# First norm's modulation formed per channel tile, and the first four FFN column tiles accumulated contraction-outermost

## The chip, the cores and the metric

One core of a Trainium2 chip runs the whole program in one launch. The metric is device time in microseconds (us) of that core; the time before is the median of three runs.

## The reference

A two-layer backbone over 512 tokens of width 1024: 256 context tokens, modulated by the condition `c_ctx`, then 256 latent tokens, modulated by `c`. Each layer is a half-step SwiGLU FFN, three parallel mixers (S5, attention, RWKV-7) with gates and an output projection, and a second half-step FFN. What matters here is the very first sub-layer:

```python
m = silu(cond) @ w_ada + b_ada              # nine vectors of 1024 per layer and condition
def norm_modulate(x, w, shift, scale):
    return rms_norm(x, w) * (1.0 + scale) + shift
def ffn_half(x, norm_w, shift, scale, gate, w1, w3, w2):
    h = norm_modulate(x, norm_w, shift, scale)
    return x + 0.5 * gate * ((silu(h @ w1) * (h @ w3)) @ w2)
```

The first norm needs two of the nine vectors (shift and scale, 2048 columns of `w_ada`, 8 MB) before the first product can be formed. The other seven are formed later, as background work.

## The kernel before

Activations lie channel-major: 8 tiles of 128 channels on the partitions, 512 tokens in the free dimension (0 to 255 context, 256 to 511 latent). All large products use float32r operands split in a high and a low part, so one product of a 128x128 weight tile is three matmuls (`mm3`, L889 to L891: high*high, high*low, low*high). Weights come as units of 128x512 numbers (256 KB) through the SP queue (`wunit`, L876; load L882); ScalarE makes the high part `wh` (L884), VectorE the low part `wl` (L885). Four raw and seven split buffers rotate.

The FFN (`ffn`, L1081) runs over two halves of 11 column tiles. For a column tile `f` it forms `p1` (w1) and `p3` (w3), each by `dense` (L896): one PSUM bank, 8 channel tiles in turn, 24 matmuls. Then Silu, a product and a split into `ghi`, `glo` (L1102 to L1105). After 11 tiles come 8 output tiles against w2 (33 matmuls each). Background work is handed out by `side()` once per column tile: from the fourth on, 56 modulation tiles of VectorE (`ada_tile`, L948: a 128x1024 row tile times the condition, summed, L962, once per condition) and 62 steps of the S5 preparation (`s5_prep`, VectorE, POOL, ScalarE). The first load of that preparation (`s5lam`, L496) is tied to the load of the last weight unit of its column tile.

Within one engine the order of instructions is fixed when the program is built: a planner goes through the program and places what is ready by its own estimate, the program's order breaking ties (`schedule_with_timeline_sim=True`). Each engine then works strictly in that order.

The start, in `ffn` with `before`:
- `first` (L1178) spreads the two conditions over all partitions by matmuls with 2 rows (`cbp`, L1190) and Silu (`cb`, L1191).
- `norm_first` (L1006) squares the 8 tiles of `xT` on ScalarE (L1013), adds them up on POOL (L1014), sums over channels with four matmuls of one column (`nss`, L1016), takes the root on POOL (`rs`, L1019), spreads it by transposes (`nrb`, L1021), copies it (L1023), and multiplies all 8 tiles by it on POOL (L1024).
- `ada_start` (L976) forms the modulation vectors: the scale of channel tiles 0 to 3 and then 4, 5 on TensorE, the two conditions as stationary columns and `w_ad0` moving (`ap`, L989), then back to channel-major (L997, L999); the shift of tiles 0 to 5 and both vectors of 6 and 7 on VectorE (10 row tiles, 20 instructions `aj`, L962).
- Then per channel tile: modulation (L1029, two instructions), high part (L1030) on ScalarE, low part (L1031) on VectorE.
- The first weight units are held back behind the load of row tile 6 (`K.after`, L959, L882).

PSUM has four pairs of banks: `mm` and `pa` for the dense products, `px` and `pc` for the rest.

Of the kernel before, what the change touches and what calls it, by code (L numbers as in the profile page):

```python
# [20 lines left out]
def rwkv_load(K, L):  # L21
# [8 lines left out]
    # derived: 1-mu, .5mu, .5w0, .5a0, .5ka, 1-.5ka , rkblk  # L30
# [22 lines left out]
class Rwkv:  # L53
    """One layer of the RWKV mixer. Channels of two heads (q: pair, par: which of the pair) lie on the
    128 partitions; direction 1 is kept in reversed token order within each 256-token half."""
    def __init__(s,K,L,W,last):
# [6 lines left out]
        # tags of the serial part: a tag's buffers are handed out in the order of the program  # L63
# [3 lines left out]
        s.ZL=[p.tile([128,2,4,4,128],F32,name=f"ZL{L}{par}",tag=f"ZL{par}") for par in range(2)]   # half, dp, slot, cols  # L67
        s.AM=p.tile([128,2,4,4,128],F32,name=f"AM{L}",tag="AM")
        s.BT=p.tile([128,2,4,4,128],F32,name=f"BT{L}",tag="BT")
        s.et=p.tile([128,2,2,2,4],F32,name=f"et{L}",tag="et")     # half, d, q, slot  # L70
        s.kd={}
        s.XV={}; s.hops=[]     # s.hops: last matmul of each step of the serial part

    def feat(s,t,ps):
        """f tile t (r0 r1 k0 k1 v0 v1 wa g) from PSUM: centred shift and lerp"""
# [3 lines left out]
        h0=1 if s.last and t in (0,1,7) else 0; C=slice(h0*256,512)     # the last layer reads r and g of the latent tokens only  # L79
# [19 lines left out]
    def kknorm(s):  # L99
        """kk = k*k_k, normalised per head, times 1/sqrt(2)"""  # L100
# [22 lines left out]
    def xv(s,sl):  # L123
        """tile that holds states and values of slot sl, with its values filled in"""
# [4 lines left out]
        if sl//2 not in s.XV:  # L129
            X=s.f4([128,2,2,2,2,64],f"XV{L}{sl//2}")      # slot, par, d, q, v  # L130
# [30 lines left out]
    def piece(s,hf,d,q,th,ta):  # L161
        """chunk matrices of one half, direction and head pair: ZL, AM, BT, et"""
# [4 lines left out]
        sv=s.last and hf==0     # only the state is wanted  # L167
# [12 lines left out]
        T2=s.f2([128,2,256],f"T2{nm}")       # (beta, k), token  # L180
# [11 lines left out]
        BK=s.f2([128,4,2,64],f"BK{nm}")        # slot, (beta,k) or (k,beta), token  # L192
# [22 lines left out]
        # token-major [beta;k]*exp(tot)  # L215
# [32 lines left out]
    def solve_b(s,hf):  # L248
        """inverses of 32x32 blocks, then of the 64x64 blocks, into AM"""
# [184 lines left out]
def exp_acc(nc,pool,out,x,n,nm):  # L434
    """out = exp(x) to float32 rounding, x any, [128,n] tiles"""
# [13 lines left out]
    # 2^k through the exponent field  # L449
# [6 lines left out]
def sincos_acc(nc,pool,sn,cs,x,n,nm):  # L456
    """sin and cos of x by reduction to [-pi,pi], half angle Taylor and one doubling"""
# [18 lines left out]
    V.tensor_mul(s,s,r)          # sin(x/2)  # L476
# [8 lines left out]
def cmul(E,ore,oim,ar,ai,br,bi,t1,t2):  # L485
    """o = a*b complex with engine E elementwise; outs may alias nothing"""
# [3 lines left out]
def s5_prep(K,L,pool):  # generator; each step is one piece of background work  # L490
    """Discretised matrices of layer L, written to DRAM scratch per group of two pairs."""
# [931 lines left out]
```

## Time and profile before

| | |
|---|---|
| runs | 2367.77, 2358.55, 2364.77 us |
| median | 2364.77 us |
| span of the profiled execution | 2365.0 us (no time of its own is listed beside the span) |
| TensorE busy | 2248.8 us, 95% of the span |
| VectorE, ScalarE, POOL busy | 67%, 45%, 29% |
| mean granted TensorE clock | 0.956 |
| moved by DMA | 363.46 MB, mean 154 GB/s |

Times in the profile are counted from the start of the span. The granted clock is a share of 2.4 GHz (0.50 is 1.2 GHz); where no change has been recorded yet it stands at 1.00. A float32 matmul appears as two MATMUL rows, a float32r matmul as one. A merged row "start, length, engine, line, operation, xN" covers N instructions that follow one another on their engine.

### The profile page before, as it was taken

The numbers are of one execution on the slowest core, as the hardware profiler recorded it, in microseconds if no ns is written. First come the engines' busy times: TensorE is split into PE (matmuls) and PEld (weight loads), VectorE is DVE, ScalarE is ACT, GpSimd is POOL, SyncE is SP. The second block draws the span as 40 slices with busy tenths as digits, with TensorE's granted clock in tenths as the row PEclk, the third lists the DMA queues.
The fourth block names the chain that finished last, engine by engine and source line by source line (L and its number), as shares of the span: only waits on it lengthen the run. The fifth ranks groups of instructions, "written<-read, shape, count | busy, mean of one in ns | idle before, by whom it ended". The sixth has DMA issues, their size and how long they took to land.

```text
span 2365.0 us, 40987 instructions
## 1 busy us (share of the span) xinstructions
PE 2248.8 (95%) x14438; PEld 1931.5 (82%) x14438; DVE 1578.8 (67%) x3212; ACT 1057.8 (45%) x2469; POOL 692.9 (29%) x1182
## 2 busy tenths in 40 slices
PE   7998979998999999899999999999999889998999
PEld 3876767876789999688888888888887778888999
DVE  7885469569854776876647656535547985687655
ACT  4445453343335554553223345525335424665554
POOL 5039960045511323783000002402003453231000
PEclk8999989999869999999999999999999978999999
DMA  7565467354332264445535525535524543265664
GB/s 255 169 204 172 133 203 239 117 165 132 92 98 81 95 209 140 155 169 193 170 118 178 154 88 187 189 118 174 174 74 140 163 113 109 75 212 191 178 190 131
DMA packets 216578, 363.46 MB, mean 154 GB/s; under 512 B 50482, under 2 KB 85426, under 8 KB 216244
## 3 DMA queue, kind: packets, MB, share of 16 engines
q1 hardware_dynamic: 214356, 360.09, 48.7%
q8 instruction: 113, 1.85, 0.3%
q10 hardware_dynamic: 2016, 0.76, 0.1%
q14 instruction: 93, 0.76, 0.1%
HBM read 320.90 MB, written 39.86 MB: 153 GB/s over the span
## 4 chain that ended last, share of the span: by engine, by line
PE 71%; DVE 10%; POOL 8%; issue 5%; DMA 3%; ACT 3%; SPq 0%; DVEq 0%; POOLq 0%; ACTq 0%
PE p L891 15%; PE p L890 15%; PE p L889 15%; PE pg L891 3%; PE pg L889 3%; PE pg L890 3%; POOL s5w L487 1%; DVE s L962 1%; POOL s5u L487 1%; POOL s5u L488 1%; POOL s5w L488 1%; PE pv L256 1%; PE pS L261 1%; PE pq L890 1%; DVE s5w L661 1%
## 5 line engine op out<-in xcount | busy, mean ns | idle before, releaser
L885 DVE TENSOR_TENSOR wl<-wr,wh 128x512 fp32r<-128x512 f32 (+1 forms) x568 | 385.7, 682 | 361.5 <-ACT wh L884 331.6
L884 ACT ACTIVATE wh<-wr 128x512 fp32r<-128x512 f32 (+1 forms) x568 | 347.5, 617 | 544.2 <-PE p L890 460.4
L889 PE MATMUL p<-hhi,wh 128*128 128x512 f32 (+1 forms) x1440 | 518.2, 363 | 15.4 <-ACT wh L884 11.5
L890 PE MATMUL p<-hlo,wh 128*128 128x512 f32 (+1 forms) x1440 | 520.8, 363 | 1.5 <-DVE hlo L1071 1.2
L891 PE MATMUL p<-hhi,wl 128*128 128x512 f32 (+1 forms) x1440 | 520.4, 362 | 0.6 <-DVE wl L885 0.6
L889 PEld LDWEIGHTS p<-hhi,wh 128*128 128x128 f32 x1440 | 274.2, 192 | 58.7 <-ACT wh L884 13.6
L891 PEld LDWEIGHTS p<-hhi,wl 128*128 128x128 f32 x1440 | 275.6, 192 | 43.8 <-DVE wl L885 2.4
L890 PEld LDWEIGHTS p<-hlo,wh 128*128 128x128 f32 x1440 | 275.6, 191 | 42.9 <-DVE hlo L1071 1.9
L962 DVE SCALAR_TENSOR_TENSOR s<-ad,cb 128x1024 f32<-128x1024 f32 x224 | 275.9, 1234 | 2.6
L889 PE MATMUL p<-ghi,wh 128*128 128x512 f32 (+1 forms) x704 | 249.5, 355 | 4.1 <-ACT ghi L1104 4.1
L890 PE MATMUL p<-glo,wh 128*128 128x512 f32 (+1 forms) x704 | 249.4, 355 | 0.5 <-DVE glo L1105 0.5
L891 PE MATMUL p<-ghi,wl 128*128 128x512 f32 (+1 forms) x704 | 249.1, 354 | 0.0
L891 PE MATMUL pg<-hhi,glpg 128*128 128x256 f32 x512 | 158.2, 309 | 9.1 <-DVE glpg L874 8.4
L889 PE MATMUL pg<-hhi,ghpg 128*128 128x256 f32 x512 | 156.3, 305 | 0.1
L889 PEld LDWEIGHTS p<-ghi,wh 128*128 128x128 f32 x704 | 133.7, 190 | 22.9 <-ACT ghi L1104 5.0
L890 PE MATMUL pg<-hlo,ghpg 128*128 128x256 f32 x512 | 152.1, 297 | 0.0
L890 PEld LDWEIGHTS p<-glo,wh 128*128 128x128 f32 x704 | 133.6, 190 | 19.1 <-DVE glo L1105 0.9
L891 PEld LDWEIGHTS p<-ghi,wl 128*128 128x128 f32 x704 | 133.5, 190 | 18.1 <-issue 0.2
L873 ACT ACTIVATE ghpg<-wrpg 128x256 fp32r<-128x256 f32 x176 | 72.0, 413 | 123.3 <-PE pg L890 101.7
L874 POOL TENSOR_TENSOR glpg<-wrpg,ghpg 128x256 fp32r<-128x256 f32 x88 | 69.2, 789 | 171.5 <-ACT ghpg L873 161.4
L891 PEld LDWEIGHTS pg<-hhi,glpg 128*128 128x128 f32 x512 | 104.7, 205 | 16.6 <-DVE glpg L874 10.2
L889 PEld LDWEIGHTS pg<-hhi,ghpg 128*128 128x128 f32 x512 | 104.7, 204 | 6.1 <-issue 0.7
(716 smaller groups left out, 4494.1 us busy)
## 6 DMA issues: line engine op xcount, KB each, us to landing
wr<-w SPq DMA_DIRECT2D x480, 256.0 KB
ad<-w_ada SPq DMA_DIRECT2D x138, 512.0 KB
wrpg<-w_g SPq DMA_DIRECT2D x96, 256.0 KB
wr<-w SPq DMA_DIRECT2D x64, 192.0 KB
s5tab<-s5tabd SPq DMA_DIRECT2D x16, 640.0 KB
s5tabd<-s5tb SPq DMA_DIRECT2D x8, 768.0 KB
wrpf<-w_f SPq DMA_DIRECT2D x24, 256.0 KB
gd<-gt SPq DMA_DIRECT2D x24, 256.0 KB
```

The costliest lines, as they stand in the source:

```text
L256: for m in range(16): h=nc.tensor.matmul(pv[R,m,:],AMv[H,m,c:c+32],T[H,m,:],start=True,stop=True)
L261: for m in range(16): h=nc.tensor.matmul(pS[R,m,:],VT[R,m,:],D[R,m,:],start=True,stop=True)
L487: E.tensor_mul(t1,ar,br); E.tensor_mul(t2,ai,bi); E.tensor_sub(ore,t1,t2)
L488: E.tensor_mul(t1,ar,bi); E.tensor_mul(t2,ai,br); E.tensor_add(oim,t1,t2)
L873: K.nc.scalar.activation(hi,raw,AF.Copy)
L874: (K.nc.gpsimd if eng=='pool' else K.nc.vector).tensor_sub(lo,raw,hi.bitcast(F32))
L884: nc.scalar.activation(hi[:,0:n],raw,AF.Copy)
L885: (nc.gpsimd if eng=='pool' or i<=K.PW else nc.vector).tensor_sub(lo[:,0:n],raw,hi[:,0:n].bitcast(F32))
L889: nc.tensor.matmul(ps,lhi,rhi,start=start,stop=False)
L890: nc.tensor.matmul(ps,lhi,rlo,start=False,stop=False)
L891: nc.tensor.matmul(ps,llo,rhi,start=False,stop=stop)
L962: nc.vector.scalar_tensor_tensor(j,raw,1.0,K.cb[:,v,:],op0=ALU.mult,op1=ALU.mult,accum_out=K.M[L][:,v,ct:ct+1])
```

## The change

- `w_ad0` is repacked: 8 loads of 1 MB, one per channel tile, each with shift and scale of that tile for all 1024 rows. The 10 row tiles on VectorE are gone, and `ada_start` with them.
- New `ada_rows`: per channel tile 8 float32 matmuls with 256 moving columns. The stationary operand is 32 columns wide (two conditions, the rest zero); the products go to PSUM partitions 0, 32, 64, 96 in turn, so four groups of 32 array columns each sum a quarter of the rows. A ScalarE copy and two small matmuls against `c_sel` add the four quarters and turn them channel-major; two small VectorE instructions give shift and scale.
- The sums of squares go through TensorE for every channel tile (8 times four one-column matmuls) in place of the POOL additions.
- The norm is as in the other norms: per channel tile and condition one VectorE instruction with the spread root read from PSUM, ScalarE for the high part, VectorE for the low part. The POOL multiplication is gone.
- The products of the first two column tiles (w1 and w3 of f=0 and f=1) are formed together: four banks (`mm`, `pa`, `mm`, `pa`), channel tile outermost, 12 matmuls per channel tile. The first four weight units are loaded behind `xT` and the first `w_ad0`, the second four at channel tile 3. `K.after` is gone.

The diff, cut (it also strips comments and docstrings throughout, left out here):

```diff
-def ada_start(K,k,ct):
...
-def norm_first(K,before):
...
+def ada_rows(K,k,raw):
+    nc=K.nc; M=K.M[0]
+    ps=K.px([128,256],f"ar{k}")
+    for r in range(2):
+        for j in range(4):
+            i=r*4+j; nc.tensor.matmul(ps[j*32:j*32+32],K.ct[:,i,:],raw[:,i*256:i*256+256],start=r==0,stop=r==1)
+    row=(K.st,K.tn)[k%2][:,4096:4352]
+    nc.scalar.activation(row,ps,AF.Copy)
+    pc=K.pc([128,2,2],f"ac{k}")
+    for c in range(2): nc.tensor.matmul(pc[:,c],row[:,c*128:c*128+128],K.sel0,start=True,stop=True)
+    nc.vector.tensor_scalar(M[:,:,k],pc[:,0],K.bada[0][:,k:k+1],None,op0=ALU.add)
+    nc.vector.tensor_scalar(M[:,:,8+k],pc[:,1],K.bada1[:,k:k+1],K.nw[0][:,k:k+1],op0=ALU.add,op1=ALU.mult)
+
+def first_products(K):
...
+    for k in range(8): nc.sync.dma_start(xT[:,k],I['xT'][:,k])
+    load(0)
+    src=[I[w][0,0,f] for f in (0,1) for w in ('w1','w3')]
+    us=[[wunit(K,u[:,0:512],512)] for u in src]
+    for k in (1,2,3): load(k)
+    ps=K.mm([128,4],"nss0")
+    for k in range(8):
+        sq=p.tile([128,2,256],F32,name=f"nsq0{k}",tag="nt",bufs=2).rearrange("p a t -> p (a t)")
+        nc.scalar.activation(sq,xT[:,k],AF.Square)
+        for t in range(4): nc.tensor.matmul(ps[:,t:t+1],sq[:,t*128:(t+1)*128],K.ones1,start=k==0 and t==0,stop=k==7,skip_group_check=True)
+    ada_rows(K,0,raw(0))
...
+    pr=K.pc([128,512],"nrb0")
...
+    bank=[mm(K,f"p{'13'[i%2]}00{i//2}",alt=i%2==1) for i in range(4)]
+    for k in range(8):
+        if k==3:
+            for u,w in zip(src,us): w.append(wunit(K,u[:,512:1024],512))
+        tt=p.tile([128,2,256],F32,name=f"nt0{k}",tag="nt",bufs=2)
+        for h,v,s in ((0,1,slice(0,256)),(1,0,slice(256,512))):
+            t=tt[:,h]; a=M[:,v,8+k:9+k]; b=M[:,v,k:k+1]
+            nc.vector.scalar_tensor_tensor(t,xT[:,k,s],a,pr[:,s],op0=ALU.mult,op1=ALU.mult)
+            nc.scalar.activation(K.hhi[:,k,s],t,AF.Identity,bias=b)
+            nc.vector.scalar_tensor_tensor(K.hlo[:,k,s],t,b,K.hhi[:,k,s].bitcast(F32),op0=ALU.add,op1=ALU.subtract)
+        if k<7: ada_rows(K,k+1,raw(k+1))
+        if k+4<8: load(k+4)
+        for ps,w in zip(bank,us):
+            hi,lo=w[k//4]; j=slice(k%4*128,k%4*128+128)
+            mm3(nc,ps,hi[:,j],lo[:,j],K.hhi[:,k],K.hlo[:,k],k==0,k==7)
+    return bank
...
-def ffn(K,L,i,n0,side,before=None):
+def ffn(K,L,i,n0,side,first=False):
...
+    if first: bank=first_products(K)
...
-            if ff==0 and not n0 and not before:
+            if first and ff<2: p1,p3=bank[2*ff:2*ff+2]
+            elif ff==0 and not n0:
...
+    wa=inp['w_ada'][0][:,0:2048].reshape(8,128,2,8,128)
+    A['w_ad0']=cc(wa.transpose(3,1,0,2,4)).reshape(8,128,2048)
```

## Rows read from the trace of the kernel before

**Rows 1.** Page: part 1, part 4 (chain by engine), part 5 (weight split, mean ns).
```profile
PE 2248.8 (95%) x14438; PEld 1931.5 (82%) x14438; DVE 1578.8 (67%) x3212; ACT 1057.8 (45%) x2469; POOL 692.9 (29%) x1182
...
PE 71%; DVE 10%; POOL 8%; issue 5%; DMA 3%; ACT 3%; SPq 0%; DVEq 0%; POOLq 0%; ACTq 0%
...
L885 DVE TENSOR_TENSOR wl<-wr,wh 128x512 fp32r<-128x512 f32 (+1 forms) x568 | 385.7, 682 | 361.5 <-ACT wh L884 331.6
```

**Rows 2.** Windows of 20 us: length, then PE, PEld, DVE, ACT, POOL busy, clock, DMA, GB/s.
```profile
40.00:60.00 20.00, 17.66 (x67) 13.93 (x68) 19.95 (x40) 11.65 (x21) 1.07 (x1) 0.82 0.68 232
...
100.00:120.00 20.00, 20.00 (x89) 16.54 (x89) 19.64 (x52) 6.51 (x11) 0.00 (x0) 1.00 0.68 217
...
160.00:180.00 20.00, 16.42 (x68) 12.99 (x66) 12.49 (x27) 13.51 (x52) 18.09 (x37) 0.92 0.52 169
...
280.00:300.00 20.00, 16.32 (x70) 13.01 (x68) 6.75 (x13) 2.44 (x5) 14.14 (x34) 0.91 0.25 73
```

**Rows 3.** Groups by line, PE: first row 0 to 60 us, second 0 to 80.
```profile
L889 PE MATMUL p<-hhi,wh 128*128 128x512 f32 x23 | 9.8, 456 | 4.0 <-ACT wh L884 4.0
...
L889 PE MATMUL p<-hhi,wh 128*128 128x512 f32 x53 | 20.5, 418 | 4.0 <-ACT wh L884 4.0
```

**Rows 4.** Timeline, 0 to 60 us: start, length, engine, line, operation.
```profile
0.84 0.95 POOL L547 MEMSET s5WT<- 128x1024 f32 x1
...
3.00 7.18 PE L1190 MATMUL cbp<-cr,ident 2*128 2x512 f32 x8 [3.00 <-DMA cr<-c]
...
20.47 1.05 PE L1016 MATMUL nss<-ones,nacc 128*128 128x1 f32 x8 [1.79 <-POOL nacc L1014]
...
22.93 1.98 POOL L1019 TENSOR_TENSOR rs<-ms,mhalf 128x4 f32<-128x4 f32 x1 [2.51 <-DVE ms L1018]
...
24.96 0.65 PE L1021 MATMUL nrb<-ident,rs 128*128 128x128 f32 x4 [1.63 <-POOL rs L1019]
...
25.55 1.05 PE L999 MATMUL apc<-ident,tn 2*128 2x2 f32 x8
...
26.33 14.75 POOL L1024 TENSOR_TENSOR tn<-xT,st 128x512 f32<-128x512 f32 x8 [1.42 <-ACT st L1023]
...
33.79 2.28 DVE L962 SCALAR_TENSOR_TENSOR aj<-ad,cb 128x1024 f32<-128x1024 f32 x1
...
38.21 1.74 DVE L1031 TENSOR_TENSOR hlo<-nt,hhi 128x512 fp32r<-128x512 f32 x1
...
43.57 0.79 PE L891 MATMUL p<-hhi,wl 128*128 128x512 f32 x1 [0.63 <-DVE wl L885]
```

**Rows 5.** Windows, PE alone: length, busy, clock, DMA share, GB/s.
```profile
27.00:28.00 1.00, 1.00 (x3) 0.50 0.90 362
...
33.00:35.00 2.00, 0.00 (x0) 1.00 0.82 238
...
37.00:38.00 1.00, 1.00 (x2) 0.50 0.00 0
```

**Rows 6.** Timeline: float32 matmuls to one column group (L989) and to two (L295).
```profile
10.11 3.31 PE L989 MATMUL ap<-st,cT 128*2 128x512 f32 x4
...
14.24 1.88 PE L989 MATMUL ap<-st,cT 128*2 128x512 f32 x4 [0.82 <-DMA st<-w_ad]
...
705.68 0.69 PE L295 MATMUL p<-XV,ZL 128*64 128x64 f32 x16
```

**Rows 7.** Single lines: ns min/median/max, first and last start, forms.
```profile
L295 PE MATMUL p<-XV,ZL x256: 222/222/271, 705.7 to 2068.1; 128*64 128x64 f32 x128
...
L1064 DVE SCALAR_TENSOR_TENSOR ntf<-xT,M,nrbf x40: 466/475/481, 1028.3 to 2172.1; 128x256 f32<-128x256 f32 x40
```

**Rows 8.** Windows of 5 us, columns as in the windows of 20 us.
```profile
10.00:15.00 5.00, 4.18 (x7) 0.52 (x7) 4.33 (x4) 2.38 (x4) 3.95 (x4) 1.00 1.02 417
```

**Rows 9.** Timeline of SP, then of POOL: first load and first long run of S5.
```profile
66.63 0.43 SPq L496 DMA_DIRECT2D s5lam<-s_lam  x1
...
156.14 0.76 POOL L487 TENSOR_TENSOR s5u<-s5B,s5f 128x64 f32<-128x64 f32 x1 [9.14 <-DVE s5t L526]
```

More of the change, by code (lines that the diff above doesn't have):

```diff
@@ L946, in prods, with ada_tile @@
             mm3(K.nc,ps[:,s],h,l,hhi[:,k,s],hlo[:,k,s],k==0 and c==n0,k==nk-1 and c+w==z)
-def ada_tile(K,L,ct,vecs,fin=True):
+def ada_tile(K,L,ct,vecs):
     nc=K.nc
@@ L955, in ada_tile @@
         for v in range(2): nc.scalar.activation(K.cb[:,v,:],K.cb[:,v,:],AF.Silu)
-    if not fin and ct<2: raw=K.ff.tile([128,1024],F32,name=f"ad{L}_{ct}",tag="fs",bufs=2)
-    else: raw=K.adp.tile([128,1024],F32,name=f"ad{L}_{ct}",tag="adr",bufs=K.ADR)
-    with K.tc.issue_after(K.po) if L and ct<K.ADR else nullcontext(): i=nc.sync.dma_start(raw,K.I['w_ada'][L,ct])
-    if not fin and ct==K.CA: K.after=i.ins
+    raw=K.adp.tile([128,1024],F32,name=f"ad{L}_{ct}",tag="adr",bufs=K.ADR)
+    with K.tc.issue_after(K.po) if L and ct<K.ADR else nullcontext(): nc.sync.dma_start(raw,K.I['w_ada'][L,ct])
     for v in vecs:
-        j=K.junk if fin else K.adp.tile([128,1024],F32,name=f"aj{L}_{ct}_{v}",tag="adj",bufs=1)
-        nc.vector.scalar_tensor_tensor(j,raw,1.0,K.cb[:,v,:],op0=ALU.mult,op1=ALU.mult,accum_out=K.M[L][:,v,ct:ct+1])
-    if fin and ct%8==7:
+        nc.vector.scalar_tensor_tensor(K.junk,raw,1.0,K.cb[:,v,:],op0=ALU.mult,op1=ALU.mult,accum_out=K.M[L][:,v,ct:ct+1])
+    if ct%8==7:
         j=ct//8
@@ L974, in ada_fin @@
         nc.vector.tensor_scalar(M[:,v,s],M[:,v,s],0.5,None,op0=ALU.mult)
-def ada_start(K,k,ct):
+def ada_rows(K,k,raw):
     nc=K.nc; M=K.M[0]
-    if k not in (0,4): return
-    n=4 if k==0 else 2; w=n*128; c0=8+k; ps=K.pa([2,512],f"ap{k}")
-    for u in range(n):
-        raw=K.st[:,(k+u)*1024:(k+u)*1024+1024] if k+u<5 else K.tn[:,8:10,:].rearrange("p a t -> p (a t)")
-        if k==0 and u<2:
-            for h in (4*u,4*u+2): nc.sync.dma_start(K.xT[:,h:h+2],K.I['xT'][:,h:h+2])
-        nc.sync.dma_start(raw,K.I['w_ad0'][k+u])
-        for i in range(1024//w):
-            j=u*(1024//w)+i
-            nc.tensor.matmul(ps[:,0:w],ct[:,j,:],raw[:,i*w:i*w+w],start=j==0,stop=j==7)
-        ada_tile(K,0,k+u,(0,1),fin=False)
-    def fin(a,b,scale):
-        m=M[:,:,a:b]; sh=[128,2,b-a]
-        nc.vector.tensor_add(m,m,K.bada[0][:,a:b].unsqueeze(1).to_broadcast(sh))
-        if scale: nc.vector.scalar_tensor_tensor(m,m,1.0,K.nw[0][:,a-8:b-8].unsqueeze(1).to_broadcast(sh),op0=ALU.add,op1=ALU.mult)
-    fin(k,k+n,False)
-    row=K.tn[0:2,10,:]
-    nc.scalar.activation(row[:,0:w],ps[:,0:w],AF.Copy)
-    pc=K.pa([128,4,2],f"apc{k}")
-    for i in range(n): nc.tensor.matmul(pc[:,i,:],row[:,i*128:i*128+128],K.ident[0:2,0:2],start=True,stop=True)
-    nc.vector.tensor_copy(M[:,:,c0:c0+n],pc[:,0:n].rearrange("p i v -> p v i"))
-    fin(c0,c0+n,True)
-    if k==4:
-        for i in (6,7):
-            for c in (i,8+i): ada_tile(K,0,c,(0,1),fin=False); fin(c,c+1,c>7)
@@ L1006, in norm_first @@
-def norm_first(K,before):
-    nc=K.nc; xT=K.xT; p=K.nrm
-    before(0)
-    acc=p.tile([128,2,256],F32,name="nacc0",tag="nacc",bufs=1).rearrange("p a t -> p (a t)")
+    ps=K.px([128,256],f"ar{k}")
[6 more added lines that the diff above has]
+    for c in range(2): nc.tensor.matmul(pc[:,c],row[:,c*128:c*128+128],K.sel0,start=True,stop=True)
@@ new lines, in ada_rows @@
+    nc.vector.tensor_scalar(M[:,:,k],pc[:,0],K.bada[0][:,k:k+1],None,op0=ALU.add)
+    nc.vector.tensor_scalar(M[:,:,8+k],pc[:,1],K.bada1[:,k:k+1],K.nw[0][:,k:k+1],op0=ALU.add,op1=ALU.mult)
+def first_products(K):
+    nc=K.nc; xT=K.xT; p=K.nrm; I=K.I; M=K.M[0]
+    K.st=K.ff.tile([128,11,512],F32,name="st",tag="ghi",bufs=1).rearrange("p a t -> p (a t)")
+    K.tn=K.ff.tile([128,11,512],F32,name="tn",tag="glo",bufs=1).rearrange("p a t -> p (a t)")
+    K.ct=K.tn[:,4608:4864].rearrange("p (a b) -> p a b",a=8); K.sel0=K.tn[:,4864:4866]; K.bada1=K.tn[:,4896:4904]
+    ct=K.st[:,4608:4624].rearrange("p (a b) -> p a b",a=8)
+    nc.sync.dma_start(ct,I['cT']); nc.scalar.dma_start(K.sel0,I['c_sel'])
+    nc.gpsimd.memset(K.ct,0.0); nc.scalar.activation(K.ct[:,:,0:2],ct,AF.Silu)
+    nc.vector.tensor_scalar(K.bada1,K.bada[0][:,8:16],1.0,None,op0=ALU.add)
+    raw=lambda k: (K.st,K.tn)[k%2][:,k//2%2*2048:k//2%2*2048+2048]
+    load=lambda k: nc.sync.dma_start(raw(k),I['w_ad0'][k])
+    for k in range(8): nc.sync.dma_start(xT[:,k],I['xT'][:,k])
[4 more added lines that the diff above has]
+    ps=K.mm([128,4],"nss0")
@@ L1011, in norm_first @@
     for k in range(8):
-        sq=acc if k==0 else p.tile([128,2,256],F32,name=f"nsq0{k}",tag="nt",bufs=2).rearrange("p a t -> p (a t)")
+        sq=p.tile([128,2,256],F32,name=f"nsq0{k}",tag="nt",bufs=2).rearrange("p a t -> p (a t)")
         nc.scalar.activation(sq,xT[:,k],AF.Square)
-        if k: nc.gpsimd.tensor_add(acc,acc,sq)
-    ps=K.px([128,4],"nss0")
-    for t in range(4): nc.tensor.matmul(ps[:,t:t+1],acc[:,t*128:(t+1)*128],K.ones1,start=True,stop=True)
+        for t in range(4): nc.tensor.matmul(ps[:,t:t+1],sq[:,t*128:(t+1)*128],K.ones1,start=k==0 and t==0,stop=k==7,skip_group_check=True)
@@ L1079, in resid @@
         nc.vector.scalar_tensor_tensor(K.xT[:,m,s],(ps[1-v] if isinstance(ps,tuple) else ps)[:,s],g,K.xT[:,m,s],op0=ALU.mult,op1=ALU.add)
-def ffn(K,L,i,n0,side,before=None):
+def ffn(K,L,i,n0,side,first=False):
     nc=K.nc; I=K.I; p=K.ff
     sub=0 if i==0 else 2
-    if before:
-        K.st=p.tile([128,11,512],F32,name="st",tag="ghi",bufs=1).rearrange("p a t -> p (a t)")
-        K.tn=p.tile([128,11,512],F32,name="tn",tag="glo",bufs=1)
-        norm_first(K,before)
+    if first: bank=first_products(K)
     else: norm(K,L,sub,n0,f"f{L}{i}")
@@ L1136, in build @@
         K.ident=cst.tile([128,128],F32,name="ident")
-        K.ct=cst.tile([128,8,2],F32,name="cT")
         K.mhalf=cst.tile([128,64],F32,name="mhalf"); nc.gpsimd.memset(K.mhalf,-0.5)
@@ L1192, in first @@
                 with tc.tile_pool(name="s5p",bufs=1) as sp:
-                    ffn(K,0,0,0,mkside(weave(ada_tasks(0,range(16,72),1),prep_tasks(0,sp),22,3)),before=lambda k: ada_start(K,k,ct))
+                    ffn(K,0,0,0,mkside(weave(ada_tasks(0,range(16,72),1),prep_tasks(0,sp),22,3)),first=True)
                 after_a(0)
```

15 lines of the change are left out of this document (removed).

## Prediction

> **What bounds the kernel now.** I read the page first, then the windows, then the start by timeline. The page [rows 1]: TensorE is busy 95% of the span and is 71% of the chain that ended last, so what counts is when the products start and where TensorE waits. The windows of 20 us [rows 2] show two kinds of stretch in the first FFN. From 100 to 120 us TensorE is busy throughout, 89 matmuls in 20 us, 0.2247 us each, and VectorE runs 19.64 of 20 with the background work: both are full. From 160 us POOL is busy 18.09 of 20, TensorE loses 3.6 us there and 3.7 between 280 and 300, where it waits behind the S5 preparation.
>
> The start is the stretch that the change rewrites. The groups by line give three lines of dense products with 23 matmuls each by 60 us [rows 3], 69 in all. At 0.2247 us the 96th, the last of the first two column tiles, comes at 60 + 27 x 0.2247 = **66.1 us**. After the change the same 96 are the ones formed contraction-outermost, so the time of the 96th is the measure: what it moves, all behind it moves, if the FFN passes it on.
>
> Why they are late [rows 4]: the products that follow one another start at 43.57, though the spread root stood at 25.61. In between POOL multiplies eight tiles (14.75 us to 41.1) while VectorE shares the time, so a modulation pass of VectorE takes 2.28 us there and a low part 1.74, and each queues behind the other. The median of the runs, 2364.77, stands 0.2 under the span of 2365.0, so I work from 2365. Some 0.5%, 11.8 us, is what a measurement can tell from no change; the three runs shown lie 9.2 us apart.
>
> **Part by part.** *Removed:* 20 modulation passes of VectorE, eight POOL multiplications (14.75 us), seven POOL additions, 16 ScalarE modulations and their copies. All of it lay between 10 and 60 us, and it is what held the products back. SP issues 16 loads for xT and the modulation where it issued 20, of the same 10 MB, and the first weight units move from behind the sixth row tile to behind xT and the first 1 MB. No SP load waits for VectorE's row tiles any more.
>
> *Added, in the order in which TensorE meets it.* (a) The spreading of the conditions stays: 3.00 to 10.18 us [rows 4]. (b) The sums of squares: 8 x 4 matmuls, 64 in the profile's count. Eight of them took 1.05 us, so 64 take 8.4 us at that clock and 16.8 at half of it. The clock at the start was the lower one: four matmuls of 512 columns took 3.31 us at 10.11 and 1.88 at 14.24 [rows 6]. So TensorE is through with them between 10.2 + 8.4 = 18.6 and 27.0; ScalarE's squares and xT (2 MB at 417 GB/s [rows 8], 5 us) end well before. I take the middle, 22.8, since the rise before 14.24 came with wide matmuls that the one-column ones do not replace. (c) Mean, root and transposes: 1.98 + 0.65 [rows 4] and hand-overs, 3.0 us, VectorE now being free: 25.8. (d) The first channel tile: two VectorE instructions of 0.475 [rows 7], then ScalarE's high part and VectorE's low part of the second half, counted at the same length: 2.0 us with hand-overs. First dense product at **27.8**.
>
> (e) The modulation by TensorE: 16 matmuls of 256 columns per channel tile. In one column group 512 columns took 0.47 us (1.88 / 4), so 256 take 0.235 and 16 in series 3.8 us. With two groups alternating, 16 matmuls of 64 columns took 0.69 us [rows 6], of which 0.22 is the last one's length [rows 7]: 0.031 us from start to start, where one group by the same price gives 0.059. Two groups ran side by side; for four the bounds are 0.95 us (all four) and 3.8 (none). I take 0.95, as the trace shows no sign of a series. With it go four small matmuls at 1.05 / 8 = 0.13 [rows 4], so 1.5 us a channel tile. The page "TensorE: Matmul & The Clock Gate" of the Trainium skill (Part 3, measured speedup) gives 2.38 times for three column groups; an estimate from it for four, at the same loss, is 3.2 times and 1.2 us, which would add 1 us to the sum.
>
> (f) How many of these lie on the path: at 417 GB/s 1 MB is 2.5 us. xT is in at about 9, then the first `w_ad0` at 11.5, weights 14, and channel tiles 1 to 3 at 16.5, 19 and 21.5. TensorE has 5 us free between 22.8 and 27.8, so four of the eight are done before the first product, if the planner hoists them; it does hoist what is ready (the S5 memsets of a later column tile run at 0.84 us [rows 4]). Four remain: 6.0 us. (g) 96 products: 21.6 us. (h) The clock: it was down at 27, 37 and again until shortly after 47 in the kernel before, after stretches like 33 to 35 us without a matmul [rows 5]. Dense products ran from 43.57 and the clock rose near 47.1, half of 3.6 us lost: 1.8 us.
>
> Sum: 27.8 + 21.6 + 6.0 + 1.8 = **57.2 us**, 8.9 earlier than 66.1.
>
> *What lies beside it.* VectorE per channel tile: four instructions of 0.475, two small ones, one weight split of 0.68 [rows 1]: 3.0 us, hidden beside 2.7 us of products and 1.5 of modulation; with no modulation left to form VectorE would set the pace by 0.3 us a tile. ScalarE has two high parts, a copy and a split, less than that. DMA: channel tile 7 lands after 12 MB, at about 34 us, TensorE wants it after 50. The row copy in `ada_rows` is a new wait, ScalarE between two matmul groups, some 0.6 us; behind it on TensorE stand the products of the tile before if the planner puts them there, else 0.6 x 4 is added, 2.4 us. The root stays in one `pc` bank, the small matmuls share the other; they wait for a VectorE read of 0.2 us. Next late: the S5 preparation. Its first load is tied to the fourth column tile's weights (66.63 us, long run on POOL from 156.14 [rows 9]) and its VectorE steps lie between the background passes, so I move it with the products.
>
> Forecast: 2365.0 - 8.9 = **2356 us**. Its own bounds: (b) at full clock and no loss in (h) give 51.2 and 2350; (b) at half clock, or two groups at a time, 61 and 2360.
>
> **Rivals.** *DMA alone bounds the start.* The clock stays up from 13 us, rows overlap with one-column matmuls: last `w_ad0` 34 + its rows and norm 4 + 12 products 2.7 = 41 us, 25 earlier, 2340; between that and 2350, I name 2345. For it: DMA is full at the start, share 1.02 [rows 8]; against: 96 products after a root at 25 us do not fit before 47.
>
> *Column groups in series.* 2.85 us more for each of four rows: 68.6 us, 2367. Against it the 0.031 us above.
>
> *The gain is given back.* The time lost from 160 us hangs on POOL, busy 18.09 of 20 [rows 2]. If its chain starts at 156 as before, because VectorE at 19.64 of 20 cannot prepare it sooner, the products wait there: 2365. Against: VectorE's queue holds the same order, only earlier.
>
> *Slower: the clock stays at half through the first products.* The place is TensorE between 27 and 85 us; it decides if the products come in bursts of 12 with waits between, as each channel tile waits for its modulation. Then (b) ends at 27.0, the first product is at 32, and (e) and (g) double: 32 + 2 x 27.6 = 87 us, 21 later, 2386. For it: the first two products of the kernel before, at 37 us, ran at clock 0.50 with nothing behind them [rows 5]. Against: once rows are ahead, 12 products are 2.7 us without a gap. The same page of the Trainium skill, section "Loop structure matters more than you think", calls a load waited for in each contraction step the bad loop, since TensorE then runs cold; by that rule this case decides, and the trace bears it out only for gaps like that from 33 to 35 us.
>
> **How the numbers follow.** Forecast 0.35, a third of it below 2353; DMA bound 0.30; series 0.08; given back 0.15; half clock 0.12. Faster by over 0.5%: 0.30 + 0.12 = 0.42. Within: 0.23 + 0.08 + 0.15 = 0.46. Slower: 0.12. The range takes in the DMA bound and the series case, 2341 to 2369, and leaves out the half clock. The forecast's own range is 2350 to 2362.
>
> **What would show it.** The count of dense products by 60 us should be near 105 rather than 69. The first `nss` group should end near 23, the root's transposes near 26, the first dense product near 28. `ada_rows` matmuls should start in fours. POOL's long S5 run should start near 147. Wrong, if the 96th product is after 66, if the clock reads 0.50 between 35 and 55, if starts lie 0.2 apart within a modulation group, or if the start moves and the FFN's end does not.

## The result, and the profile after

The changed kernel takes **2384.05 us** (median of six runs, 2382.82 to 2389.09); the kernel before, beside it, 2367.38 (six runs, 2358.55 to 2379.30). The ratio is 1.0072, with an interval of 1.0047 to 1.0096: slower by 16.7 us, outside the predicted range. The profiled run took 2383.67 us with a span of 2381.9, 16.9 over the span of before.

The page of the changed kernel, its first part, against [rows 1]: TensorE has 172 MATMUL rows more (14610 for 14438) and is busy 20.4 us longer; VectorE and POOL are relieved.

```profile
PE 2269.2 (95%) x14610; PEld 1952.3 (82%) x14610; DVE 1560.6 (66%) x3199; ACT 1053.5 (44%) x2466; POOL 664.9 (28%) x1168
```

Where the 16.9 us arise is read from windows cut at the same places of the work in both: the start of the 96th, 1584th, 1800th, 4000th, 7000th, 7250th and 9000th dense product. The columns are the window, its length, busy time and instructions of PE, PEld, DVE, ACT and POOL, the granted clock, DMA share and GB/s. First the kernel before:

```profile
0.00:66.00 66.00, 49.38 (x159) 27.28 (x160) 49.23 (x77) 30.18 (x55) 30.66 (x26) 0.90 0.70 246
66.00:453.30 387.30, 357.03 (x1585) 290.95 (x1584) 282.38 (x643) 170.85 (x494) 167.21 (x372) 0.96 0.56 180
...
492.40:1067.20 574.80, 540.47 (x4249) 469.87 (x4248) 413.88 (x898) 267.00 (x605) 258.55 (x396) 0.92 0.42 131
1067.20:1739.40 672.20, 670.67 (x3118) 559.82 (x3117) 389.26 (x684) 267.13 (x613) 81.50 (x183) 1.00 0.51 158
...
1781.50:2213.90 432.40, 404.44 (x3581) 363.46 (x3580) 317.81 (x666) 220.88 (x505) 143.30 (x188) 0.92 0.48 146
```

The same windows of the changed kernel:

```profile
0.00:69.00 69.00, 64.25 (x332) 43.89 (x333) 24.64 (x64) 25.90 (x52) 3.71 (x12) 0.98 0.63 235
69.00:456.20 387.20, 355.20 (x1585) 288.86 (x1584) 282.26 (x643) 170.95 (x494) 167.28 (x372) 0.97 0.56 180
...
495.30:1068.60 573.30, 536.48 (x4249) 466.46 (x4248) 417.80 (x896) 267.12 (x607) 256.78 (x398) 0.93 0.41 132
1068.60:1740.80 672.20, 670.67 (x3117) 559.63 (x3116) 391.35 (x687) 266.32 (x612) 81.39 (x180) 1.00 0.51 158
...
1783.00:2230.60 447.60, 415.72 (x3580) 373.33 (x3580) 318.32 (x666) 221.52 (x505) 144.19 (x188) 0.88 0.46 141
```

The start loses 3.0 us where 8.9 were to be gained. The first FFN is as long as before (387.2 for 387.3), and so are the FFNs between the mixers (672.2). The mixers of layer 0 are 1.5 shorter, those of layer 1 **15.2 longer**, and the rest is equal within 0.3. So most of the loss lies 1700 us behind the change, in a stage that no line of it touches. (These are single profiles; one program profiled twice, among the experiments, has its mixers alike within 0.4 us and its 96th product 1.6 us apart.)

**The start.** The timeline of TensorE in the changed kernel (start, length, engine, line, operation, count; PEld is the loading of the stationary operand):

```profile
3.15 5.46 PE L1187 MATMUL cbp<-cr,ident 2*128 2x512 f32 x6 [3.15 <-DMA cr<-c]
8.53 3.49 PEld L1011 LDWEIGHTS nss<-ones,nsq 128*128 128x128 f32 x16 [1.50 <-issue]
8.53 3.57 PE L1011 MATMUL nss<-ones,nsq 128*128 128x1 f32 x16
12.03 2.07 PE L1187 MATMUL cbp<-cr,ident 2*128 2x512 f32 x2
14.03 3.57 PE L1011 MATMUL nss<-ones,nsq 128*128 128x1 f32 x16
17.53 1.93 PE L980 MATMUL ar<-st,tn 128*32 128x256 f32 x16
...
25.61 3.57 PE L1011 MATMUL nss<-ones,nsq 128*128 128x1 f32 x16
...
33.46 0.65 PE L1017 MATMUL nrb<-ident,rs 128*128 128x128 f32 x4
...
36.49 1.85 PE L889 MATMUL p<-hhi,wh 128*128 128x512 f32 x4
38.27 1.94 PE L980 MATMUL ar<-st,tn 128*32 128x256 f32 x16
40.14 0.50 PE L890 MATMUL p<-hlo,wh 128*128 128x512 f32 x1
```

The sums of squares come in four groups of 16 rows (two rows are one matmul) and 3.57 us, 0.223 us a row, and end at 29.2 us; the root stands on POOL at 30.6, but its transposes wait in TensorE's queue behind modulation rows until 33.46 (POOL's rows, from the same timeline):

```profile
29.54 1.01 POOL L1015 TENSOR_TENSOR rs<-ms,mhalf 128x4 f32<-128x4 f32 x1 [26.30 <-DVE ms L1014]
```

The first product starts at 36.49, against 36.9 in the kernel before; the stream of products starts at 40.1 against 43.57 [rows 4] and then carries the rows of four channel tiles between its groups of 12. The single line of the high*high products has fewer by 60 us (20 where [rows 3] has 23), and after that it does not catch up (48 by 80 us for 53). Three such lines make 60 dense products by 60 us, where the prediction looked for 105:

```profile
L889 PE MATMUL p<-hhi,wh x20: 389/397/628, 36.5 to 56.5; 128*128 128x512 f32 x20
...
L889 PE MATMUL p<-hhi,wh x48: 389/389/628, 36.5 to 79.4; 128*128 128x512 f32 x48
```

Windows of 4 us of the changed kernel show what limits it there: DMA is full until 42 us, later than the 34 reckoned, and then nearly idle up to 50 us, while TensorE, which still waits for 1.6 us between 34 and 38, is busy throughout from there on.

```profile
34.00:38.00 4.00, 2.40 (x13) 1.76 (x12) 4.00 (x13) 2.20 (x5) 0.00 (x0) 0.84 1.00 402
38.00:42.00 4.00, 4.00 (x25) 2.15 (x25) 2.25 (x6) 1.29 (x3) 0.00 (x0) 0.73 0.95 383
42.00:46.00 4.00, 4.00 (x22) 3.33 (x21) 0.60 (x3) 0.00 (x0) 0.00 (x0) 1.00 0.07 26
46.00:50.00 4.00, 4.00 (x32) 2.56 (x30) 1.79 (x6) 0.91 (x2) 0.00 (x0) 1.00 0.01 4
```

(Where no change of the clock has been recorded yet, a window shows 1.00; up to 36 us the lengths of the matmuls tell that it was the lower level.) In the stage windows above the same is seen as busy time: 332 matmuls and 64.25 of 69 us after, 159 and 49.38 of 66 before. The kernel before waited for VectorE and POOL; this one is held by TensorE's own added work.

**The mixers of layer 1.** Of the 15.2 us, 11.3 are TensorE's busy time (415.72 for 404.44, for the same number of matmuls), at a mean clock of 0.88 for 0.92, and 3.9 are waits. Windows of 10 us in the middle of the stage show the first kind, in the kernel before:

```profile
2000.00:2010.00 10.00, 10.00 (x192) 9.44 (x187) 3.52 (x7) 3.31 (x8) 4.74 (x5) 0.67 0.20 67
2010.00:2020.00 10.00, 9.99 (x133) 8.99 (x131) 7.45 (x15) 7.11 (x14) 3.45 (x3) 0.84 0.23 69
2020.00:2030.00 10.00, 10.00 (x127) 8.93 (x128) 8.00 (x15) 4.41 (x11) 4.26 (x6) 1.00 0.22 67
2030.00:2040.00 10.00, 10.00 (x127) 8.87 (x126) 6.74 (x17) 5.34 (x17) 2.04 (x3) 1.00 0.31 93
```

and in the changed one:

```profile
2000.00:2010.00 10.00, 10.00 (x141) 9.26 (x139) 3.39 (x8) 3.55 (x8) 1.76 (x2) 0.50 0.17 53
2010.00:2020.00 10.00, 9.75 (x135) 9.11 (x133) 3.50 (x7) 4.51 (x9) 4.14 (x5) 0.50 0.19 49
2020.00:2030.00 10.00, 10.00 (x107) 9.09 (x105) 4.61 (x8) 2.18 (x6) 3.47 (x4) 0.50 0.15 47
2030.00:2040.00 10.00, 10.00 (x96) 8.59 (x94) 8.53 (x16) 6.01 (x14) 3.96 (x4) 0.82 0.20 67
```

TensorE waits for nearly nothing in either, but from 2000 to 2030 the changed kernel runs at 1.2 GHz throughout. (The same window holds somewhat different parts of the stage in the two.) The instructions do not stand in the same order: of the last 11800 instructions of TensorE, 2851 stand in another place than in the kernel before, nearly all of them in the two mixers (counted in the two programs). The orders of the other engines, and which buffer of a rotation an instruction gets, move along with it. Nothing in the code there was edited. The planner that fixes the order goes by its own estimates of time, and with another start it places what is ready in the mixers differently; the experiments show that a delay of the start is enough.

### The profile page after: what moved, and what is told of

The parts are those of the page before. It is cut to its first block, busy times and chain, and to the rows that moved or that the text cites. A ratio compares the mean times of both kernels' runs of the same rounds, so it can differ in the third digit from the quotient of the medians.

```text
span 2381.9 us, 41318 instructions
## 1 busy us (share of the span) xinstructions
PE 2269.2 (95%) x14610; PEld 1952.3 (82%) x14610; DVE 1560.6 (66%) x3199; ACT 1053.5 (44%) x2466; POOL 664.9 (28%) x1168
## 4 chain that ended last, share of the span: by engine, by line
PE 74%; DVE 8%; POOL 7%; issue 4%; DMA 3%; ACT 2%; SPq 1%; DVEq 0%; ACTq 0%; POOLq 0%
PE p L889 15%; PE p L890 15%; PE p L891 15%; PE pg L891 3%; PE pg L889 3%; PE pg L890 3%; POOL s5w L487 1%; POOL s5u L487 1%; PE pS L261 1%; POOL s5w L488 1%; POOL s5u L488 1%; DVE s L959 1%; PE pv L256 1%; DVE s5w L661 1%; PE pq L890 1%
## 5 line engine op out<-in xcount | busy, mean ns | idle before, releaser
L884 ACT ACTIVATE wh<-wr 128x512 fp32r<-128x512 f32 (+1 forms) x568 | 347.0, 618 | 539.7 <-PE p L890 463.8
```

Source lines behind the costliest of these rows:

```text
L884: nc.scalar.activation(hi[:,0:n],raw,AF.Copy)
```

## The experiments

Two theories were put against each other. One: the start costs 3 us, and the planner's other order of the mixers costs the rest. The other: the new start itself costs everything (its loads, buffers or the clock), or the clock decides by itself and the order is without weight. Four kernels take both starts with both kinds of order. The planner's order is moved by a short delay ahead of the first load; nothing computed is changed by it (`xT` is overwritten by its load):

```diff
+xf=K.xT.rearrange("p a t -> p (a t)"); nc.gpsimd.memset(xf[:,0:N],0.0); nc.gpsimd.tensor_copy(K.ident,xf[:,0:128])
 nc.sync.dma_start(K.ident,I['c_ident'])
```

**After, mixers as before** (the changed kernel, N=1328; 32 of the last 11800 TensorE instructions differ from the kernel before).

> The changed kernel with one POOL memset of 1328 columns ahead of the first load, which delays the start by some 1.5 us; with it the planner puts the two mixers in the order of the kernel before. Theory A (the planner's order of the mixers makes most of the loss, the start only 2.9 us): 2367 + 1.5 + 2.9 = 2371 us, 13 less than the changed kernel without the delay. Theory B (the mixers lose at run time, through clock and transfers, whatever their order): 2384 + 1.5 = 2385 us. Both: the last product of the first FFN starts about 4.4 us after that of the kernel before.

**Before, the same delay** (N=1328; its own order of the mixers).

> The kernel before with the same memset; its mixers keep their order. Both theories: 2367 + 1.5 = 2368 to 2369 us. The difference of the run before this one to it is the price of the changed start alone, order of the mixers equal: A says 2.9 us, B says 16.

**Before, other mixers** (N=2228; 3404 of 11800 differ).

> The kernel before with a memset of 2228 columns, some 2.3 us of delay, at which the planner reorders both mixers. A: the time leaves 2369 by up to 15 us either way, and the difference arises between 600 and 1000 us and after 1880 us, with the first FFN's end only 2.3 us later. B: 2367 + 2.3 = 2369 to 2370 us.

**After, other mixers** (the changed kernel, N=728; 3642 of 11800 differ).

> The changed kernel with a memset of 728 columns, some 0.9 us of delay, at which the planner makes a third order of the mixers. A: the time differs from 2385 by several us, with the first FFN's end at 2.9 + 0.9 us behind that of the kernel before. B: 2385 us.

Measured, beside the kernel before (2369.92 us, 27 runs). The last four columns are read from each profile at the same products as above:

| kernel | median, us | ratio (interval) | 96th | 1584th | mixers layer 0 | mixers layer 1 |
|---|---|---|---|---|---|---|
| before | 2369.92 | | 66.0 | 453.3 | 574.8 | 432.4 |
| after | 2384.05 | 1.0072 (1.0047 to 1.0096) | 69.0 | 456.2 | 573.3 | 447.6 |
| after, mixers as before | 2365.59 | 0.9988 (0.9967 to 1.0009) | 71.8 | 458.2 | 565.1 | 436.0 |
| before, same delay | 2378.72 | 1.0034 (1.0010 to 1.0058) | 73.4 | 460.8 | 570.8 | 439.5 |
| before, other mixers | 2396.25 | 1.0082 (1.0049 to 1.0115) | 77.5 | 463.8 | 578.5 | 448.9 |
| after, other mixers | 2383.23 | 1.0060 (1.0035 to 1.0086) | 71.9 | 458.3 | 565.2 | 453.7 |

(The profile of before is the one shown ahead of the prediction; the after row was measured beside a before of 2367.38.)

In layer 1 the order decides. With the changed start, the two delayed kernels have the 96th product at the same time (71.8 and 71.9) and differ by 17.6 us by the medians and 19.4 by the profiled spans, of which layer 1 gives 17.7 and the FFNs between the mixers 3.0. With the start of before, the two delayed kernels differ by 17.5 by the medians and 20.2 by the spans: 7.7 in layer 0, 9.4 in layer 1, and 3.0 from the longer delay at the 1584th product (4.1 at the 96th). Stage windows of the two kernels with the changed start, the one with the mixers as before first:

```profile
1776.70:2212.70 436.00, 408.15 (x3580) 366.57 (x3579) 317.46 (x666) 221.02 (x505) 142.47 (x188) 0.91 0.46 145
```

```profile
1778.40:2232.10 453.70, 425.18 (x3580) 379.39 (x3579) 316.38 (x666) 224.06 (x505) 139.90 (x188) 0.87 0.45 139
```

The same instructions in another order have TensorE busy 17.0 us longer, at 0.87 for 0.91.

Several numbers missed. The kernel before with the delay came out about 9 us above what it was expected to take. The delayed load of `ident` holds back the spreading of the conditions by 6.4 us (9.38 for 3.00), the 96th product comes 7.4 us later, and 7.5 of these are there at the 1584th; that accounts for 7.5 of the 8.8 us over before. The delay of 2228 columns put off the first FFN's end by 10.5 us, not 2.3, and the time went 26 us up, not up to 15. The changed kernel with the mixers as before took 5 us less than theory A gave it (2371). Its difference to the kernel before with the same delay, the price of the changed start alone, was to be 2.9 us (A) or 16 (B) and came out at -13.1: neither. Its start is 2.6 shorter at the 1584th product, its mixers are 9.2 shorter in the profiles although the order of TensorE's instructions there is the same, and its mean clock was 0.959 for 0.951 (the last section sets the clock apart). The changed kernel with other mixers lies within 2 us of the 2385 that B gave it, so alone it decides nothing; the pair does.

The clock by itself does not explain layer 1. The kernel before with the same delay has the same mean clock there, 0.89, and nearly the same busy time of TensorE as the kernel with the squares on VectorE and another order, shown further down, and is 11.5 us shorter, by less waiting:

```profile
1785.00:2224.50 439.50, 413.82 (x3581) 371.97 (x3580) 317.93 (x666) 221.74 (x505) 142.62 (x188) 0.89 0.46 144
```

Over all profiles, those of the kernels below too, layer 1 took 429.7 to 439.5 us where the order is that of the kernel before, and 442.8 to 453.7 elsewhere. Layer 0 took 565.1 to 578.0 with the order of before and 565.2 to 585.0 in others: there a price of the order is not shown.

**Squares on VectorE.** The start has a suspect of its own, the 32 one-column matmuls (64 rows). This kernel sums the squares on VectorE and leaves four of them; with the delay of 1328 columns its mixers stand nearly as before (397 of 11800 differ).

```diff
...
-for t in range(4): nc.tensor.matmul(ps[:,t:t+1],sq[:,t*128:(t+1)*128],K.ones1,start=k==0 and t==0,stop=k==7,skip_group_check=True)
+if k: nc.vector.tensor_add(acc,acc,sq)
+for t in range(4): nc.tensor.matmul(ps[:,t:t+1],acc[:,t*128:(t+1)*128],K.ones1,start=True,stop=True)
```

> The changed kernel with the squares added up on VectorE and four one-column matmuls in all (as the kernel before did on POOL), and a memset of 1328 columns ahead of the first load, at which the planner orders the mixers nearly as in the kernel before. Theory C (the 64 one-column matmuls at half clock are what made the first product late): the transposes of the root end near 21 rather than 34.1 us, delay included, and the 96th product starts 9 to 13 us before that of the run with the same delay and the squares on TensorE (71.8 us), so at 59 to 63 us; the time is 2355 us. Rival D (the loads of the modulation and the order of TensorE's queue set the 96th product, whatever the root does): the 96th product within 3 us of 71.8, the time 2364.

Measured: 2368.88 us (2364.27 to 2375.19) beside a before of 2368.00 (19 runs), ratio 1.0004 (0.9982 to 1.0026). The timeline of its TensorE:

```profile
17.47 1.87 PE L1013 MATMUL nss<-ones,nacc 128*128 128x1 f32 x8
...
22.18 1.12 PE L1019 MATMUL nrb<-ident,rs 128*128 128x128 f32 x4
...
24.86 1.20 PE L889 MATMUL p<-hhi,wh 128*128 128x512 f32 x4
```

The transposes of the root end at 23.3 us, 2 later than expected, and the 96th product comes at 60.5 us, 11.3 earlier than with the same delay and the squares on TensorE: that is what summing them there cost. But the time is 3.3 us above that kernel, not 11 below: layer 0 takes 571.8 for 565.1 and layer 1 443.5 for 436.0, with the 397 instructions of the latter placed differently. A gain of 11 us at the start was lost in the mixers; the 6.7 us of it in layer 0, where the order is the same, are not explained.

**Contraction inner.** The changed kernel with its first two column tiles formed one after the other, as before, in a single run. The loads of their weight units move with it (the first four start at 9.27 us for 7.10, the next at 26.85 for 17.29):

```diff
-us=[[wunit(K,u[:,0:512],512)] for u in src]
...
-for ps,w in zip(bank,us):
-    hi,lo=w[k//4]; j=slice(k%4*128,k%4*128+128)
-    mm3(nc,ps,hi[:,j],lo[:,j],K.hhi[:,k],K.hlo[:,k],k==0,k==7)
...
-if first and ff<2: p1,p3=bank[2*ff:2*ff+2]
-elif ff==0 and not n0:
+if ff==0 and not n0 and not first:
```

> The changed kernel without the contraction-outermost products: f=0 and f=1 bank by bank as before, all else as changed. If that order of products is worth what the prediction took for granted, the 96th product starts 8 us or more after 69.0 us; under rival D, modulation rows first and products afterwards, it comes within 3 us of 69.0. The mixers' order differs, so the time says nothing.

**Before with the contraction outermost**, the other way round, in a single run (the second modulation group goes to the other PSUM pair, so that the four banks are free). Its first weight units are loaded from 13.57 us, ahead of modulation loads, where the kernel before loads them from 25.72. What the next passage and the title count as four column tiles are the w1 and w3 products of the first two column tiles:

```diff
...
+us=[[wunit(K,u[:,0:512],512)] for u in src]
+bank=[mm(K,f"p{'13'[i%2]}00{i//2}",alt=i%2==1) for i in range(4)]
...
+for ps,w in zip(bank,us):
+    hi,lo=w[k//4]; j=slice(k%4*128,k%4*128+128)
+    mm3(nc,ps,hi[:,j],lo[:,j],K.hhi[:,k],K.hlo[:,k],k==0,k==7)
```

> The kernel before, its modulation and norm untouched, with the first four column tiles contraction-outermost (the second modulation group in px and pc banks so that four banks are free). If the modulation part of the change is what costs and the product order what gains, the 96th product starts before 63 us; if the product order is worth nothing by itself, at 64 to 68 us (66.0 in the kernel before).

Measured: 2384.46 us with the 96th product at 66.7, 2.3 earlier than in the changed kernel; and 2396.96 us with the 96th at 69.0, 3.0 later than in the kernel before. The second lies outside both of its ranges. Its root is already 2.0 us late ahead of any product (its transposes start at 26.95, [rows 4] has 24.96):

```profile
26.95 0.65 PE L1021 MATMUL nrb<-ident,rs 128*128 128x128 f32 x4 [1.64 <-POOL rs L1019]
```

So the gain that the outer contraction was taken to bring does not show at either kind of modulation. That it costs 2 to 3 us is not shown: these are single runs, the order of the loads moves along, and one program's 96th product came at 71.8 and at 70.2 us in two profiles. Both kernels have other orders of the mixers, and the times say nothing of the start: 2384.46 with the start 0.7 from before's.

**Squares on VectorE, no delay.** The same edit as above without the memset; 3525 of 11800 instructions stand elsewhere than before.

> The squares on VectorE without the delay: another order of the mixers. C: the 96th product 9 to 13 us before 69.0, so at 56 to 60 us; the end of the first FFN equally earlier than the changed kernel's. D: 66 to 69 us. The time is free by up to 15 us through the mixers' order.

Measured: 2381.06 us (2379.12 to 2388.48), ratio 1.0052 (1.0031 to 1.0073), with the first product at 21.6 us and the 96th at 58.6. The start is 7.4 earlier than in the kernel before, at the 1584th product it is 7.9, and the time is 13 above the 2368.0 of the kernel before beside it. Layer 0 takes 585.0 us. Its layer 1:

```profile
1784.30:2235.30 451.00, 415.69 (x3579) 372.70 (x3579) 323.05 (x666) 222.11 (x505) 143.71 (x188) 0.89 0.46 140
```

**Three and two rows ahead.** The pair that was to settle it: the squares on VectorE, no delay, and the modulation rows of three, or two, channel tiles formed ahead of the products. With three, the planner gives both mixers the order of the kernel before (32 of 11800 differ); with two, layer 0 has it and layer 1 does not (1341 differ).

```diff
 ada_rows(K,0,raw(0))
+ada_rows(K,1,raw(1))
+ada_rows(K,2,raw(2))
...
-if k<7: ada_rows(K,k+1,raw(k+1))
+if k<5: ada_rows(K,k+3,raw(k+3))
```

> The changed kernel with the squares summed on VectorE and with the modulation rows of three channel tiles formed ahead of the products (in place of one); nothing is delayed. Both mixers' instructions stand as in the kernel before (32 of the last 11800 of TensorE differ). Theory of two parts (start, and order of the mixers): the 96th product comes no later than in the kernel with the squares on VectorE alone (58.6 us), rather 1 to 2 us earlier, so 57 +- 1.5; the 1584th some 8 to 10 before 453.3; the layer-1 mixers take 432 to 440 us, not 447 to 454; the time is some 8 us below that of the kernel before beside it, ratio 0.9965 (0.994 to 0.999). Rival, the order is without weight and the new start itself costs time later (the mixers lose because the start's buffers or loads lie otherwise): as the kernel with the squares on VectorE and no delay, 2378 to 2383, layer-1 mixers 447 to 454. Rival, the granted clock decides by itself: anything between 2360 and 2380, with the time on the line of 1.4 us per 0.001 of clock.

> The same kernel with the rows of two channel tiles ahead in place of three: a start that is the same but for some 1 us, the layer-0 mixers in the order of the kernel before, the layer-1 mixers in another (some 1340 of the last 11800 instructions of TensorE differ). Theory (the order of the layer-1 mixers costs): 96th product at 57 to 58.6; layer-0 mixers 570 to 578 us; layer-1 mixers 443 to 454 us; the time 8 to 16 above that of the kernel with three ahead: 2368 to 2376. Rival (the order is without weight): within 3 us of the kernel with three ahead.

Measured beside a before of 2370.69 us (29 runs): three ahead **2360.58 us**, ratio 0.9955 (0.9935 to 0.9975); two ahead 2371.35, ratio 0.9991 (0.9968 to 1.0014). Start, layer 0 and layer 1 of three ahead, in windows as above:

```profile
0.00:59.30 59.30, 50.24 (x276) 31.86 (x277) 29.45 (x71) 25.74 (x52) 4.03 (x12) 0.97 0.73 274
...
484.70:1062.70 578.00, 544.22 (x4249) 473.11 (x4249) 415.21 (x898) 267.30 (x605) 258.72 (x398) 0.91 0.40 130
...
1777.00:2206.70 429.70, 402.44 (x3580) 360.41 (x3580) 320.53 (x666) 221.52 (x505) 142.29 (x188) 0.92 0.47 147
```

and of two ahead:

```profile
0.00:57.80 57.80, 48.38 (x275) 31.32 (x276) 28.82 (x71) 25.55 (x52) 3.71 (x12) 1.00 0.75 281
...
485.40:1056.90 571.50, 540.22 (x4249) 470.56 (x4248) 415.20 (x898) 267.03 (x605) 258.50 (x397) 0.92 0.41 132
...
1771.20:2223.10 451.90, 416.57 (x3581) 373.41 (x3580) 324.44 (x666) 222.29 (x505) 144.84 (x188) 0.89 0.45 140
```

Two ahead is 1.5 us earlier at the 96th product and enters layer 1 5.8 us earlier (1771.2 for 1777.0), and yet it is 10.8 us slower by the medians: layer 1, where alone the order differs, takes 451.9 for 429.7. TensorE is busy 14.1 longer there and waits 8.1 longer. The rival that the order is without weight, within 3 us, falls. Three ahead beats both kernels: 10.1 us under the before beside it, and 23 under the changed one, which was measured apart. Misses: the 1584th product was to come 8 to 10 us before that of the kernel before and came 7.6 before it; layer 1 lies 2.3 below its range; and the rows ahead were to bring the 96th product to 57, 58.5 at the latest, and it came at 59.3. The rows that are drawn ahead push the first product from 21.6 to 29.0, and there, at 1.2 GHz, a channel tile's rows take 1.93 us where they take 1.07 among the products:

```profile
19.51 1.93 PE L980 MATMUL ar<-tn 128*32 128x256 f32 x16 [0.52 <-DMA tn<-w_ad]
...
29.03 1.51 PE L889 MATMUL p<-hhi,wh 128*128 128x512 f32 x4 [0.83 <-ACT hhi L1030]
...
36.39 1.07 PE L980 MATMUL ar<-st,tn 128*32 128x256 f32 x16
```

**Mixers as before, again.** The first of these kernels once more, to see whether its higher clock is its own.

> The same kernel as the changed one with the mixers in the order of before (after plus a memset of 1328 columns), once more. If its granted clock of 0.9586 (mean of ten runs, where the kernel before had 0.9542) belongs to the kernel, the clock is 0.957 to 0.960 again and the time 2364 to 2368, some 3 us below that of the kernel before beside it. If the clock belongs to the occasion, it is that of the kernel before here, and the time is 3 to 5 us above it (the start is 5 later at the 1584th product).

Measured: 2365.83 us (2360.47 to 2386.05), ratio 0.9983 (0.9956 to 1.0010), mean clock of its ten runs 0.9564 where the kernel before beside it had 0.9527; the first ten had 0.9586 beside 0.9543. The time is in the range that was named for a clock of the kernel's own, the clock a little under it, and 0.004 above that of the kernel before both times. That it is faster than the kernel before, with a start 3 to 5 us later, is not shown: both intervals include 1. The stages belong to the program: in the two profiles layer 0 took 565.1 us both times and layer 1 436.0 and 436.4, though the 96th product came at 71.8 and 70.2.

## Why the prediction was wrong, step by step

**The sentence that failed most** stands in the part on what bounds the kernel: "what it moves, all behind it moves, if the FFN passes it on". The FFN passed it on to 0.1 us. The mixers did not: those of layer 1 took 15.2 us more, because their order is not that of the kernel before. Everything was reckoned at the edit, with the planner's order taken as given elsewhere; no rival had a reordering far behind it. Of the 16.9 us, 3.0 are the start, -1.5 layer 0 and 15.2 layer 1; pairs with nearly the same start give 17.6 (changed start, delayed) and 10.8 us (three and two rows ahead) from the order, by the medians.

The sum for the start failed too, and by itself: the 96th product came at 69.0 us where 57.2 was forecast, 3.0 later than before instead of 8.9 earlier. 8.7 of these 11.8 us are there at the first product, most of them by step (b).

**(a)** The spreading of the conditions was to end at 10.2; the planner put the first squares between, and it ended at 14.1. **(b)** The sums of squares were to end at 22.8, 27.0 at the latest. The price was right (4 x 3.57 = 14.3 us, between 8.4 and 16.8), the middle was not: the clock was the lower one nearly throughout. The bound failed because the groups do not follow one another: between 8.53 and 29.2 lie 14.3 us of squares, 2.07 of conditions and 3.9 of modulation rows. The rows that step (f) hoists for nothing are hoisted into the path of the root. **(c)** 3.0 us to the end of the transposes became 4.9, because rows stand ahead of them in TensorE's queue. **(d)** 2.0 became 2.4. The first product: 36.5 for 27.8. The kernel with the squares on VectorE, where it came at 21.6, shows that (b) was the term to look at.

**(e)** was right: 16 row matmuls take 1.07 us at the higher clock, against 3.8 in series, so four column groups do run side by side, and the rival of groups in series falls. That is 3.6 times. The page "TensorE: Matmul & The Clock Gate" of the Trainium skill (Part 3, measured speedup) has 2.38 times for three groups; the trace gives a little more than the 3.2 times estimated from it. **(f)** Four tiles of rows remained, as reckoned. **(g), (h)** 96 products, rows and clock were 29.4 us and took 32.5 from the first product; whether the outer contraction is part of these 3 us is not shown.

**DMA as the bound** is out: from 42 to 50 us its share is 0.07 and 0.01, and TensorE is full. **Given back on POOL** is out: the shift is 3.0 at the 96th product and 2.9 at the 1584th, and a gain of 7.4 is passed on as 7.9. **Half clock through the first products** has the right sign by another way: TensorE was at 1.2 GHz to about 40 us, but the products from there ran at 2.4 GHz, and the 96th came at 69, not 87. The section "Loop structure matters more than you think" of the same page of the Trainium skill has TensorE go cold where a long wait for a load stands between the matmuls. It did not decide here: the windows from 42 to 50 us have no wait and a clock of 1.00. The chance of slower, 0.12, hung on a mechanism that did not happen.

What stays open: why the clock falls for longer in one order of a mixer than in another is read from the windows, and no run takes it apart. Nor is it settled why layer 0 took from 565 to 578 us in kernels that have it in the same order, when the same program gave 565.1 us twice.

## What to carry to other kernels

Where a planner orders the program, an edit at one end can reorder the other: compare the order of instructions first, and judge an edit of a few us between programs whose untouched stages stand alike, stage by stage, before its time is believed. Work moved to the engine that is the bound was paid in full here, and at the start of this program at half the clock; the sums of squares, 32 matmuls of one column, cost 11 us where VectorE had the time to spare. A row of work that is hoisted for nothing goes into somebody's queue: look whose result is behind it.

## What was not expected of the hardware

The narrowest matmuls were the dearest for their width: each row of the one-column squares took 0.223 us at 1.2 GHz (3.57 us for 16). In them the data is the stationary operand, 128x128 numbers in float32, and its loading is busy for 3.49 of each 3.57 us, so it is likely this loading that is paid. By contrast, 16 rows of 256 columns in four column groups took 1.93 us at that level and 1.07 at 2.4 GHz, 0.12 and 0.067 each.

TensorE can be busy for 29.75 of 30 us and be granted 1.2 GHz all the while (2000 to 2030 us in the changed kernel), where another order of the same work has 2.4 GHz from 2020 on.

The mean granted clock also differs from run to run of one program: the kernel before had 0.945 to 0.962 over the runs beside all these kernels. With one slope for all runs and an offset for each kernel, 0.01 of it goes with 14.4 us; at a clock of 0.955 that gives 2368.4 us for the kernel before, 2380.3 for the changed one and 2364.5 with three rows ahead, so 11.9 of the 16.7 us lost and 3.9 of the 10.1 gained are there at an equal clock. By the same line, at a clock of 0.955, the two delayed kernels with the changed start stand at 2371.8 and 2389.2 us, those with the start of before at 2372.3 and 2392.6, three and two rows ahead at 2364.5 and 2369.7: another order costs 17.4, 20.3 (of which 3.0 are delay) and 5.2 us at an equal clock, and the 13.1 us between the two kernels that have the same order and the same delay shrink to 0.5. As the order itself moves the clock, this splits the numbers and not the causes.
